# Order of the seven down products, and four smaller moves, in a decoder layer on eight cores

## The chip, the cores and the metric

One Trainium2 chip, all 8 cores; each core has 2048 of the 16384 tokens. The metric is the device time of the slowest core in microseconds (us). Some executions fall in a slower state in which one die (cores 0 to 3 or 4 to 7), or both, gets a lower granted TensorE clock, whatever the kernel; these are left out of every comparison ("fast runs" are the others). Ratios are the mean time of one kernel's fast runs over that of the other's of the same rounds; the medians quoted are of all runs, slow ones too, so the ratios are not quite theirs.

## The reference, cut to what matters

```python
def swiglu(x, w_up, w_down):
    gate, up = jnp.split(jnp.einsum('bsd,df->bsf', x, w_up), 2, axis=-1)
    return jnp.einsum('bsf,fd->bsd', jax.nn.silu(gate) * up, w_down)

def reference(...):                      # one layer: D_MODEL 2048, D_FF 5632, SEQ 16384
    mix = token_mixer(x, ...)            # projections, dilated attention A, sliding window B, w_out
    x = layer_norm(ALPHA * x + mix, ln1_g, ln1_b)
    x = layer_norm(ALPHA * x + swiglu(x, w_up, w_down), ln2_g, ln2_b)
```

The kernel works through two halves of its tokens (st) and, in each, two halves of the inner width (g): an up stage of 22 steps, then a down stage of 8 steps. So there are four down stages; they are called first to fourth here. Each product of a pair of weight blocks with the tokens is done by a scheme of seven products in place of eight; their operands are block sums (P, Q, R) of the weights.

## The kernel before

One down step p: banks BA, BB, BC, BD of PSUM take the products, VectorE adds them into the four z tiles q11 to q22, and also makes the sums P, Q, R of the next step's weights. Products 5 and 2 use P, 1 uses Q, 7 and 6 use R; 4 and 3 use the raw weights.

```python
# slots of the raw weight tiles (1408 KB each) of steps 0 to 7
D_OFF = [WB + (24576, 13312, 0)[i] for i in (0, 1, 2, 0, 1, 2, 1, 0)]

def wdone(k, key):                       # the raw weights of a step are no longer needed
    k.wlive = [e for e in k.wlive if e[0] != key]
    wfill(k)                             # issue further loads, in order, as far as slots are free

for p in range(5 if last else KC // 2):
    ...
    nxq = load_xq(p + 1) if p < 7 else None          # z tiles of the next step, a ring of five pairs
    ...
    P("5", BB, True, True, cs)
    P("1", BD, True, True, cs)
    P("4", BA, True, True, cs)
    acc(q11, BB, ALU.subtract, True)
    acc(q22, BB, ALU.subtract, True)
    acc(q11, BD)
    acc(q22, BD)
    acc(q21, BA, ALU.add, True)
    P("2", BC, True, True, cs)
    acc(q21, BC)
    if p < 7:
        d_sums(st, g, p + 1, "P")
        d_sums(st, g, p + 1, "Q")
    elif g == 0:
        u_sums(st, FG, "P")
    P("3", BB, False, True)
    wdone(k, key)
    acc(q12, BB, ALU.add, True)
    acc(q22, BB)
    P("7", BA, False, True)
    acc(q11, BA)
    if not last:
        store(0)
    P("6", BC, False, True)
    ...
    acc(q22, BC, ALU.subtract)
    if p < 7:
        d_sums(st, g, p + 1, "R")
    ...
    if g == 1:                           # LayerNorm sums: ACT squares, GpSimd adds twice per tile
        for i, q in ((2, q21), (1, q12), (0, q11), (3, q22)):
            stats(ss, i % 2, *q)
    if not last:
        store(1)
```

The softmax here doesn't subtract the row's maximum and nothing guards it: scores larger than these inputs give would overflow.

Of the kernel before, what the change touches and what calls it, by code (L numbers as in the profile page):

```python
# [43 lines left out]


class Op:
    __slots__ = ("eng", "fn", "deps", "is_dma", "semkey", "val", "needs_inc")


class Sched:  # L50
# [28 lines left out]
    def _add(self, eng, fn, reads, writes, joins=(), semkey=None):  # L79
        idx = len(self.ops)  # L80
        deps = set()
        for b in list(reads) + list(writes) + list(joins):
            for o in b.over:
                assert not o.ws, (b.name, o.name)
        for b in reads:
            deps.update(b.ws)
            if b.psum:
                deps.update(v for e, v in b.r.items() if e != eng)
        for b in list(writes) + list(joins):
            if b.prev:  # L90
                b.base |= self._old(b, set())
                b.prev = []
        for b in writes:
            deps.update(b.ws)
            deps.update(b.r.values())
            deps.update(b.rd)
            deps |= b.base
        for b in joins:
            deps |= b.base
            deps.update(b.r.values())  # L100
            deps.update(b.rd)
        op = Op()
        op.eng = eng
        op.fn = fn
        op.deps = deps
        op.is_dma = semkey is not None
        op.semkey = semkey
        op.val = 0
        op.needs_inc = False
        self.ops.append(op)  # L110
        for b in reads:
            if op.is_dma:
                b.rd.append(idx)
            else:
                b.r[eng] = idx
        for b in writes:
            b.base = set(b.ws) | set(b.r.values()) | set(b.rd)
            b.ws = [idx]
            b.r = {}
            b.rd = []  # L120
        for b in joins:
            b.ws.append(idx)
        return idx
# [10 lines left out]
    def pool(self, fn, reads, writes, joins=()):  # L134
        return self._add("pool", fn, reads, writes, joins)

    def dma(self, q, out, in_, reads, writes, semkey, joins=()):
        eng = {"sp": self.nc.sync, "pool": self.nc.gpsimd, "act": self.nc.scalar}[q]
        return self._add(q, lambda: eng.dma_start(out=out, in_=in_), reads, writes, joins, semkey=semkey)  # L139

    def emit(self, final_wait_ops):

# [9 lines left out]
        for i, op in enumerate(self.ops):  # L152
            e = op.eng
            w = []
            for d in sorted(op.deps, reverse=True):
                dop = self.ops[d]
                if not dop.is_dma and dop.eng == e and e == "pe":
                    continue
                if know[e] >> d & 1:
                    continue  # L160
                w.append(d)
                know[e] |= done[d]
            waits.append(w)
            for d in w:
                if not self.ops[d].is_dma:
                    self.ops[d].needs_inc = True
            if op.is_dma:
                done.append(know[e] | 1 << i)
                for j, (sem, last, val) in enumerate(free[e]):
                    if know[e] >> last & 1:  # L170
                        free[e].pop(j)
                        break
                else:
                    sem, val = nsem, 0
                    nsem += 1
                op.semkey, op.val = sem, val + 16
                free[e].append((sem, i, val + 16))
            else:
                issued[e] |= 1 << i
                done.append(know[e] | issued[e])  # L180
# [188 lines left out]
def phase1(k):  # L369
# [60 lines left out]
    load_x(1, (2, 2, 4, 4, 4))  # L430
    for h in range(8):
        S_.dma("pool", wk[h], k.wk_d[h], [], [bwk[h]], "wk%d" % h)
    for q in range(4):
        S_.dma("pool", wv[:, 4 * q:4 * q + 4, 1024:1152], k.wv_d[4 * q:4 * q + 4, :, 1024:1152].rearrange("c p n -> p c n"), [], [], "wvb",
               joins=[bwvb])
    S_.dma("pool", wkb, k.wkb_d, [], [bwkb], "wkb")
    k.bvs, k.bka, k.bkb = [], [[] for _ in range(8)], []
    later = []
# [173 lines left out]
def phase2(k):  # L612
# [47 lines left out]
    def load_kv(h):  # L660
# [8 lines left out]
        vt = vt.rearrange("p (b d) -> p b d", d=128)  # L669
        col = slice(h * 128, h * 128 + 128)  # L670
        first = [True]

        def ld(out, in_):
            S_.dma("sp", out, in_, k.bvs, [bv_] if first[0] else [], "va%d" % (h % 2), joins=[] if first[0] else [bv_])
            first[0] = False
        own = k.vs_d[TOK - 128:2 * TOK, col]
        ld(vt[:, 0:17, :], own.rearrange("(b p) d -> p b d", p=128))
# [329 lines left out]
    for u in range(32):  # L1007
# [3 lines left out]
            spend = [a_S(0, 0, 2, 0), a_S(0, 0, 1, 1)]  # L1011
        b_PV(j, kq, pend)
        b_evac(j, kq)
        run(peq, 1)
        proj(u + LEAD)
        run(dveq, 4)
        if u == 3:
            load_a()
# [181 lines left out]
def phase3(k):  # L1200
# [27 lines left out]
    def stats(ss, hh, z, bz):  # L1228
        (za, bza), (qa, bqa) = ss["accs"][hh]
        if hh not in ss["started"]:  # L1230
            ss["started"].add(hh)
            S_.act(lambda: nc.scalar.activation(out=qa, in_=z, func=AF.Square), [bz], [bqa])
            S_.pool(lambda: nc.gpsimd.tensor_copy(out=za, in_=z), [bz], [bza])
            return
        sq, bsq = ss["sq"][nxt("sq", len(ss["sq"]))]
        S_.act(lambda: nc.scalar.activation(out=sq, in_=z, func=AF.Square), [bz], [bsq])  # L1236
        S_.pool(lambda: nc.gpsimd.tensor_tensor(out=za, in0=za, in1=z, op=ALU.add), [bz, bza], [bza])  # L1237
        S_.pool(lambda: nc.gpsimd.tensor_tensor(out=qa, in0=qa, in1=sq, op=ALU.add), [bsq, bqa], [bqa])  # L1238

    def finish(ss, hh, bk0, both=False):  # L1240
        (za, bza), (qa, bqa) = ss["accs"][hh]
        (mu, bmu), (rs, brs) = ss["stat"][hh]
        tb, btb = ss["tt"][nxt("tt", len(ss["tt"]))]
# [79 lines left out]

    for st in range(2):
        zz = {}
        ss = open_stats("o%d" % st, [misc(9 + i) for i in range(4)], [misc(6), misc(7)], [misc(8)]) if st == 0 else ss
        ss["started"] = set()
        if st == 0:
            open_accs(ss, "o", [misc(i) for i in range(4)])
# [102 lines left out]
    def last_pairs(st, ss, zr, xq5, load_xq, acc, bhl):  # L1432
# [13 lines left out]
        def half_sum(p, o):  # L1446
# [3 lines left out]
            S_.dve(lambda: nc.vector.tensor_tensor(out=v, in0=w[:, 0:NJ, 0:128], in1=w[:, 0:NJ, 128:256], op=ALU.subtract), [bw], [b])  # L1450
            halls[p, "6"] = ([v[:, c, :] for c in range(NJ)], b)

        def stats_dve(hh, z, bz):
            (za, bza), (qa, bqa) = ss["accs"][hh]
            sq, bsq = ss["sq"][nxt("sq", len(ss["sq"]))]
# [4 lines left out]
        SB = ((4, 6), (0, 2))  # L1460
        stat = [None, None]

        def sums_out(hh):
            b0, b1 = SB[hh]
            for (a, ba), bk in zip(ss["accs"][hh], (b0, b1)):
                S_.pe(lambda a=a, bk=bk: nc.tensor.matmul(bank(k, bk), k.onesf, a, start=True, stop=True), [ba, k.bonesf], [k.bBK[bk]])
            mu, bmu = slot("mu%dl" % hh, xslot(hh))
            stat[hh] = [(mu, bmu), None]
            S_.act(lambda: nc.scalar.activation(out=tb, in_=bank(k, b0), func=AF.Square, scale=1.0 / D), [k.bBK[b0]], [btb])
# [38 lines left out]
        for p in (5, 6, 7):  # L1508
# [30 lines left out]
            if p < 7:  # L1539
                stats(ss, 0, *q11)  # L1540
                d_sums(st, g, p + 1, "R")
        stats_dve(0, *q[7][0])()

        dv = [(0, n) for n in range(13)] + [(1, n) for n in range(11)]
# [8 lines left out]
        for i, (p, m, bk) in enumerate(((5, "3", 0), (5, "6", 2), (6, "3", 1), (6, "6", 3), (7, "3", 5), (7, "6", 7))):  # L1553
            q11, q12, q21, q22 = q[p]
            prod(p, m, bk, p == 5, True)
            if m == "3":
                acc(q12, bk)
                acc(q22, bk)
                stats(ss, 1, *q12)
                if i == 0:  # L1560
                    sums_out(0)
                    ln(2)
                    rstd(0)
                ln(2)
            else:
                acc(q22, bk, ALU.subtract)
                if p < 7:
                    stats(ss, 1, *q22)
                    ln(3)
                else:  # L1570
                    tail = stats_dve(1, *q22)
                    ln(1)
                    tail()
        sums_out(1)
        ln(3)
        rstd(1)
        pend = None
# [12 lines left out]
    for st in range(2):  # L1590
        for g in range(2):
# [125 lines left out]
            for p in range(5 if last else KC // 2):  # L1717
# [18 lines left out]
                    S_.dma("sp", k.z2s_d[n, :, st * TS:(st + 1) * TS], view(k, wslot((n + 3) % 5 * 2), 1024, F32),  # L1736
                           [xq[2 * i][1], xq[2 * i + 1][1]], bz, "z2o")
                if p == 0:
                    for i, bk in (("5", BB), ("1", BD), ("4", BA), ("2", BC)):
                        P(i, bk, True, False, range(NJ - 1))  # L1740
                cs = [NJ - 1] if p == 0 else None
                P("5", BB, True, True, cs)
                P("1", BD, True, True, cs)
                P("4", BA, True, True, cs)
                acc(q11, BB, ALU.subtract, True)
                acc(q22, BB, ALU.subtract, True)
                acc(q11, BD)
                acc(q22, BD)
                acc(q21, BA, ALU.add, True)
                P("2", BC, True, True, cs)  # L1750
                acc(q21, BC)
                if p < 7:
                    d_sums(st, g, p + 1, "P")
                    d_sums(st, g, p + 1, "Q")
                elif g == 0:
                    u_sums(st, FG, "P")
                P("3", BB, False, True)
                wdone(k, key)
                acc(q12, BB, ALU.add, True)
                acc(q22, BB)  # L1760
                P("7", BA, False, True)
                acc(q11, BA)
                if not last:
                    store(0)
                P("6", BC, False, True)
                if p == 7 and g == 0:
                    u_sums(st, FG, "Q")
                acc(q22, BC, ALU.subtract)
                if p < 7:
                    d_sums(st, g, p + 1, "R")  # L1770
                elif g == 0:
                    u_sums(st, FG, "R")
                if g == 1:
                    for i, q in ((2, q21), (1, q12), (0, q11), (3, q22)):
                        stats(ss, i % 2, *q)
                if not last:
                    store(1)
                if st == 0 and g == 1:
                    if p == 0:
# [167 lines left out]
```

## Time and profile before

Median 2862.45 us (2856.41 to 3098.93 in 3 runs). What matters of the profiled run, whose slowest core is core 4:

| | us |
|---|---|
| span; PE busy; PE idle | 2861.7; 2745.7; 116 |
| the four up stages | 262, 273, 262, 273 |
| the four down stages, first to last z add | 131.9, 141.5, 129.0, 136.3 |
| PE waits inside them | 4.9, 13.7, 2.9, 4.9 |

The way to read it: PE is busy 96% of the span, so only what makes PE wait, or makes its matmuls slower, moves the time. The timeline, the stage table and the sums of VectorE that the argument rests on are shown in the prediction. One view more, PE's waits (us in total, times, longest):

```profile
PE sp L1382 <- DVE arena L1715: 14.9, 8, 5.2
PE sp L1382 <- DVE arena L1713: 6.5, 5, 1.7
PE sp L1382 <- DVE arena L1395: 4.9, 4, 2.1
...
PE sp L1247 <- POOL arena L1237: 3.5, 1, 3.5
```

L1382 are the matmuls of the up and down stages; L1715 and L1713 are VectorE's adds into z, L1395 is the block sum P. All told, the down stages hold PE up for 26 us.

### The profile page before, as it was taken

The numbers are of one execution on the slowest core, as the hardware profiler recorded it, in microseconds if no ns is written. First come the engines' busy times: TensorE is split into PE (matmuls) and PEld (weight loads), VectorE is DVE, ScalarE is ACT, GpSimd is POOL, SyncE is SP. The second block draws the span as 40 slices with busy tenths as digits, with TensorE's granted clock in tenths as the row PEclk, the third lists the DMA queues.
The fourth block names the chain that finished last, engine by engine and source line by source line (L and its number), as shares of the span: only waits on it lengthen the run. The fifth ranks groups of instructions, "written<-read, shape, count | busy, mean of one in ns | idle before, by whom it ended". The sixth has DMA issues, their size and how long they took to land.

```text
span 2861.7 us, 41480 instructions; the slowest of 8 cores (2850.4 to 2861.7 us)
## 1 busy us (share of the span) xinstructions
PE 2745.7 (96%) x14966; PEld 1319.8 (46%) x15077; DVE 1978.0 (69%) x2707; ACT 738.3 (26%) x1077; POOL 574.3 (20%) x571
## 2 busy tenths in 40 slices
PE   6999999998999999899999999998999999999995
PEld 2445555444666444344444444443444444444442
DVE  0744555788788826688865666676888765666787
ACT  0000000676666327333200112211333200212115
POOL 4000000122111555511100000046200000000166
PEclk9999999999999999999999999999999999999997
DMA  9974113556656758799989755599899799555863
GB/s 158 187 140 101 62 54 87 114 107 131 150 131 173 208 144 209 150 148 153 157 149 190 144 87 87 99 199 200 163 173 173 123 196 178 102 89 89 158 123 118
DMA packets 250810, 400.59 MB, mean 140 GB/s; under 512 B 89072, under 2 KB 127088, under 8 KB 249840
## 3 DMA queue, kind: packets, MB, share of 16 engines
q0 software_dynamic: 94272, 186.43, 43.7%
q1 hardware_dynamic: 141936, 182.12, 22.9%
q10 hardware_dynamic: 14400, 29.37, 3.4%
q8 instruction: 123, 2.02, 0.3%
q14 instruction: 79, 0.65, 0.1%
HBM read 491.42 MB, written 97.06 MB: 206 GB/s over the span
## 4 chain that ended last, share of the span: by engine, by line
PE 79%; DMA 9%; DVE 4%; issue 4%; ACT 2%; POOL 1%; ACTq 0%; DVEq 0%; POOLq 0%; SPq 0%
PE sp L1382 47%; PE sp L482 8%; PE sp L729 7%; PE sp L469 6%; PE sp L1194 4%; DMA arena<-wdn 2%; DMA z2s<-arena 2%; DMA arena<-z2s 1%; DMA arena<-wup 1%; DMA arena<-wv 1%; DMA arena<-x1s 1%; PE sp L538 1%; POOL arena L139 1%; PE sp L771 1%; ACT arena L358 1%
## 5 line engine op out<-in xcount | busy, mean ns | idle before, releaser
L1382 PE MATMUL sp<-arena 128*128 128x512 f16 x7408 | 1606.7, 380 | 31.7 <-DVE arena L1715 14.9
L1382 PEld LDWEIGHTS sp<-arena 128*128 128x128 f16 (+1 forms) x7408 | 723.8, 98 | 915.1 <-issue 50.5
L1632 DVE TENSOR_TENSOR arena<-sp,arena 128x512 f32<-128x512 f32 (+1 forms) x348 | 236.7, 689 | 159.1 <-PE sp L1382 143.9
L1715 DVE TENSOR_TENSOR arena<-arena,sp 128x512 f32<-128x512 f32 x257 | 166.6, 683 | 99.1 <-PE sp L1382 79.6
L729 PE MATMUL sp<-arena 128*128 128x512 bf16 x976 | 227.0, 381 | 5.4 <-ACT arena L358 2.2
L139 POOL DMA_DIRECT2D arena<-wup x88 | 65.9, 749 | 791.0 <-DVE arena L1395 491.1
L1194 PE MATMUL sp<-arena 128*128 128x512 bf16 x1003 | 220.7, 379 | 3.7 <-DVE arena L1359 1.5
L482 PE MATMUL sp<-arena 128*128 128x512 bf16 x1001 | 220.1, 379 | 1.2
L451 DVE TENSOR_TENSOR arena<-sp,arena 128x384 bf16<-128x384 f32 (+1 forms) x81 | 48.1, 606 | 200.8 <-PE sp L469 119.9
L1403 DVE TENSOR_TENSOR arena<-arena 128x2048 f16<-128x2048 bf16 (+1 forms) x118 | 186.8, 1583 | 0.0
L469 PE MATMUL sp<-arena 128*128 128x384 bf16 (+1 forms) x1036 | 182.4, 337 | 0.4
L1395 DVE TENSOR_TENSOR arena<-arena 128x2048 f16<-128x2048 bf16 (+1 forms) x118 | 156.6, 1327 | 34.4 <-DMA arena<-wdn 25.0
L1237 POOL TENSOR_TENSOR arena<-arena 128x512 f32<-128x512 f32 x118 | 161.0, 1365 | 74.9 <-DVE arena L1715 49.3
L1238 POOL TENSOR_TENSOR arena<-arena 128x512 f32<-128x512 f32 x118 | 157.9, 1338 | 25.6 <-ACT arena L1236 25.6
L1666 ACT ACTIVATE arena<-sp 128x512 f32<-128x512 f32 x86 | 51.5, 598 | 421.5 <-PE sp L1382 421.5
L1194 PEld LDWEIGHTS sp<-arena 128*128 128x128 bf16 x1024 | 100.0, 98 | 124.7 <-issue 5.2
L1236 ACT ACTIVATE arena<-arena 128x512 f32<-128x512 f32 x118 | 74.5, 632 | 317.1 <-DVE arena L1715 187.8
L482 PEld LDWEIGHTS sp<-arena 128*128 128x128 bf16 x1024 | 100.1, 98 | 120.3
L1632 DVE TENSOR_TENSOR arena<-arena 128x512 f16<-128x512 f32 (+1 forms) x304 | 154.8, 569 | 0.0
L358 ACT ACTIVATE arena<-sp,arena 128x512 bf16<-128x512 f32 (+1 forms) x37 | 24.7, 668 | 504.2 <-PE sp L502 429.0
L729 PEld LDWEIGHTS sp<-arena 128*128 128x128 bf16 x1024 | 97.7, 98 | 116.3 <-issue 6.5
L469 PEld LDWEIGHTS sp<-arena 128*128 128x128 bf16 x1040 | 101.7, 98 | 79.5
(143 smaller groups left out, 2510.7 us busy)
## 6 DMA issues: line engine op xcount, KB each, us to landing
arena<-wup POOLq DMA_DIRECT2D x88, 1024.0 KB, 11.3
arena<-wdn POOLq DMA_DIRECT2D x32, 1408.0 KB, 18.8
z2s<-arena SPq DMA_DIRECT2D x48, 512.0 KB, 12.4
arena<-wob SPq DMA_DIRECT2D x32, 512.0 KB, 5.9
arena<-xres SPq DMA_DIRECT2D x32, 512.0 KB, 7.8
x1s<-arena ACTq DMA_DIRECT2D x64, 256.0 KB, 7.0
arena<-x1s SPq DMA_DIRECT2D x32, 512.0 KB, 13.6
arena<-z2s SPq DMA_DIRECT2D x32, 512.0 KB, 17.4
```

The costliest lines, as they stand in the source:

```text
L139: return self._add(q, lambda: eng.dma_start(out=out, in_=in_), reads, writes, joins, semkey=semkey)
L469: ins = nc.tensor.matmul(bank(k, bk)[:, 0:c1 - c0], x[:, kc, blk * 128:blk * 128 + 128], wv[:, kc, c0:c1], start=(kc == 0), stop=(kc == KC ...
L482: ins = nc.tensor.matmul(bank(k, bk), wk[h][:, kc, :], x[:, kc, :], start=(kc == 0), stop=(kc == KC - 1))
L729: ins = nc.tensor.matmul(bank(k, bk), w[:, kc, :], x[:, kc, :], start=(kc == 0), stop=(kc == KC - 1))
L1194: ins = nc.tensor.matmul(bank(k, bk), w[:, kc, :], y[:, kc, hh * 512:(hh + 1) * 512], start=(first and i == 0), stop=(last and i == len(kc ...
L1237: S_.pool(lambda: nc.gpsimd.tensor_tensor(out=za, in0=za, in1=z, op=ALU.add), [bz, bza], [bza])
L1238: S_.pool(lambda: nc.gpsimd.tensor_tensor(out=qa, in0=qa, in1=sq, op=ALU.add), [bsq, bqa], [bqa])
L1382: ins = nc.tensor.matmul(bank(k, bk), w, x, start=(first and i == 0), stop=(last and i == len(ws) - 1), skip_group_check=True)
L1395: S_.dve(lambda: nc.vector.tensor_tensor(out=v, in0=w[:, 0:n, :], in1=w[:, n:2 * n, :], op=ALU.add), [bw], [b])
L1403: S_.dve(lambda: nc.vector.tensor_tensor(out=v, in0=w[:, :, 0:128], in1=w[:, :, 128:256], op=ALU.subtract), [bw], [b])
L1632: S_.dve(lambda: nc.vector.tensor_tensor(out=o, in0=a, in1=b, op=op), [ba, bb], [bo])
L1715: S_.dve(lambda: nc.vector.tensor_tensor(out=v, in0=v, in1=o, op=op), [b, bo], [b])
```

## The change

The intent: let VectorE add sooner, and let GpSimd's LayerNorm sums fall between VectorE's block sums, with which they contend. Four smaller moves go with it. The core of the diff:

```diff
-                P("5"), P("1"), P("4")   | acc q11 BB, q22 BB, q11 BD, q22 BD, q21 BA
-                P("2")                   | acc q21 BC; sums P, Q
-                P("3"); wdone            | acc q12 BB, q22 BB
-                P("7")                   | acc q11 BA; store(0)
-                P("6")                   | acc q22 BC; sums R; all four stats; store(1)
                 (the lines above are shortened; those below are the new code)
+                P("5", BB, True, True, cs)
+                P("2", BC, True, True, cs)
+                acc(q11, BB, ALU.subtract, True)
+                acc(q22, BB, ALU.subtract, True)
+                P("4", BA, True, True, cs)
+                acc(q21, BC, ALU.add, True)
+                sums("P")
+                P("1", BD, True, True, cs)
+                acc(q21, BA)
+                stat(0, q21)
+                P("7", BA, False, True)
+                acc(q11, BD)
+                acc(q22, BD)
+                sums("Q")
+                P("6", BC, False, True)
+                acc(q11, BA)
+                stat(0, q11)
+                P("3", BB, False, True)
+                wdone(k, key)
+                acc(q22, BC, ALU.subtract)
+                sums("R")
+                acc(q12, BB, ALU.add, True)
+                acc(q22, BB)
+                stat(1, q12)
+                stat(1, q22)
+                if not last:
+                    store(0)
+                    store(1)
 # LayerNorm sums: the add of the square is held until the next tile
-        S_.pool(lambda: nc.gpsimd.tensor_tensor(out=qa, in0=qa, in1=sq, op=ALU.add), [bsq, bqa], [bqa])
+        flush(ss)
+        ss["pend"] = [lambda: S_.pool(lambda: nc.gpsimd.tensor_tensor(out=qa, in0=qa, in1=sq, op=ALU.add), [bsq, bqa], [bqa])]
 # out projection: two square buffers, one temporary (was: one and two)
-        ss = open_stats("o%d" % st, [misc(9 + i) for i in range(4)], [misc(6), misc(7)], [misc(8)]) if st == 0 else ss
+        ss = open_stats("o%d" % st, [misc(9 + i) for i in range(4)], [misc(6)], [misc(8), misc(7)]) if st == 0 else ss
 # B: the rotation matmul of the unit before, inside the next projection
-        run(peq, 1)
-        proj(u + LEAD)
+        proj(u + LEAD, mid=lambda: run(peq, 1))
 # the loads of one V tile share one semaphore (group), which counts up to 16 times their number
-                op.semkey, op.val = sem, val + 16
+                val += 16 * len(group)
+                for m in group:
+                    self.ops[m].semkey, self.ops[m].val = sem, val
```

Left out: the tail, where a table load moves ahead and the sums of the last tile but one go straight to PE, without an add by GpSimd.

## The prediction

> **What bounds the kernel now.** I read the page first, then the busy time by stage, then the waits of PE, then the timeline of each stage that the change touches.
>
> ```profile
> PE 2745.7 (96%) x14966; PEld 1319.8 (46%) x15077; DVE 1978.0 (69%) x2707; ACT 738.3 (26%) x1077; POOL 574.3 (20%) x571
> 1210.00:1452.00 242.00, 240.96 (x1117) 108.97 (x1116) 207.66 (x308) 74.71 (x112) 31.92 (x52) 1.00 0.94 147
> 1452.00:1591.00 139.00, 133.96 (x618) 59.94 (x617) 83.41 (x109) 1.23 (x2) 6.68 (x9) 1.00 0.95 181
> 1857.00:2017.00 160.00, 146.34 (x664) 64.98 (x663) 109.20 (x115) 21.36 (x34) 92.76 (x71) 0.98 0.94 195
> 2280.00:2414.00 134.00, 131.05 (x606) 58.73 (x605) 82.47 (x108) 0.63 (x1) 6.63 (x9) 1.00 0.91 182
> 2683.00:2795.00 112.00, 107.09 (x489) 47.81 (x487) 88.89 (x92) 14.53 (x23) 62.53 (x48) 0.98 0.70 144
> ```
>
> The first line says that PE has 116 us of idle time in 2861.7; nothing else can give much. The others are stages (start:end, length, busy us of PE, weight load, DVE, ACT, POOL, granted clock, DMA share). The second is an up stage, for comparison; the last four are the down stages, one per half of the tokens and half of the inner width. They lack 5, 14, 3 and 5 us of PE work, and the first three run with the DMA engines 91 to 95% busy. The rest of the idle time is elsewhere: 19 us at the start, some 11 in attention of group B, 13 around the end of the out projection, some 20 in the tail.
>
> A down stage is eight steps p of seven products of 11 matmuls. At 217 ns each (10.74 us per 49 in the chain) a product is 2.39 us and a step 16.7. VectorE adds each product into four z tiles and makes the block sums P, Q, R of the next step's weights. These lines of the timeline show what a step waits for:
>
> ```profile
> 1465.89 100.24 PE L1382 MATMUL sp<-arena 128*128 128x512 f16 x462 [0.96 <-DVE arena L1713]
> 1535.64 1.48 POOL L139 DMA_DIRECT2D arena<-wdn  x2 [32.49 <-PE sp L1382]
> 1554.70 1.62 DVE L1395 TENSOR_TENSOR arena<-arena 128x2816 f16<-128x2816 bf16 x1 [4.62 <-DMA arena<-wdn]
> 1473.95 1.62 DVE L1403 TENSOR_TENSOR arena<-arena 128x2816 f16<-128x2816 bf16 x1
> 1895.34 7.54 DVE L1403 TENSOR_TENSOR arena<-arena 128x2816 f16<-128x2816 bf16 x1
> 1926.17 35.22 PE L1382 MATMUL sp<-arena 128*128 128x512 f16 x154 [5.17 <-DVE arena L1715]
> ```
>
> First: step 0 begins with a wait of 0.96 us. Second and third: GpSimd issues the weights of steps 6 and 7 together (x2) when step 4 lets go of its slot, and P of step 6 (L1395) can start 19.1 us later, when the first has landed. The same pair took 17.7 us (2364.25 to 2381.96) and 21.7 us (1947.82 to 1969.58) in the other two stages. Fourth and fifth: the same sum R takes 1.62 us alone and 7.54 us while GpSimd runs the LayerNorm sums back to back. Sixth: PE idles 5.17 us for a z tile loaded late, and its next 9 matmuls start every 0.43 us, then every 0.21: such an idle costs about 1.9 us more.
>
> **What the Trainium skill says.** "SBUF — State Buffer", Who interferes with whom: a VectorE instruction with two SBUF inputs contends with a GpSimd instruction that reads SBUF. The 1.62 against 7.54 us agrees. "TensorE: Matmul & The Clock Gate", Part 1: an idle window of about 3.4 us halves the clock. The trace agrees after 5.17 us idle, and shows no such start after 2.06. "DMA: Bandwidth & Descriptors", Issuing engines are not separate DMA queues: all queues interleave on the same 16 engines. The 17.7 to 21.7 us for one weight tile in the busy stages agree; in the last stage, with those queues quiet, both tiles of the pair were through in about 22 us.
>
> **The change part by part.**
>
> *Rotation of B inside the next projection.* It removes PE's waits on the bias copy of ACT (L358): 4.2 us at L362 and 2.2 at L729. But the period is not set by PE:
>
> ```profile
> 573.18 1.93 ACT L778 ACTIVATE arena<-sp 128x1024 bf16<-128x1024 f32 x2
> 574.99 0.70 ACT L834 ACTIVATE arena<-sp,arena 128x512 f32<-128x512 f32 x1
> 575.78 0.63 ACT L835 ACTIVATE arena<-arena 128x512 f32<-128x512 f32 x1
> 576.51 1.01 DVE L838 TENSOR_TENSOR arena<-sp,arena 128x512 bf16<-128x512 f32 x1 [0.61 <-ACT arena L835]
> 577.67 0.63 ACT L824 ACTIVATE arena<-arena 128x512 f32<-128x512 bf16 x1 [1.26 <-DVE arena L838]
> 578.21 0.67 ACT L358 ACTIVATE arena<-sp,arena 128x512 bf16<-128x512 f32 x1
> 578.78 1.93 ACT L778 ACTIVATE arena<-sp 128x1024 bf16<-128x1024 f32 x2
> ```
>
> From 573.18 to 578.78 each starts when the one before ends: a closed loop of ACT and DVE of 5.60 us, while PE alone needs 5.32 (its period before the loop has caught up, 523 to 535 us). The order on ACT does not change, so the loop stays; PE will wait for L838, whose bank PV overwrites, instead of L358. Worth 0.3 us.
>
> *V semaphore group.* The order of instructions shows that the first PV of each A head goes from six or seven DMA semaphores to one. In the trace that PV starts 0.75 us after the matmuls before it at the beginning of a head, 0.48 otherwise: 8 x 0.27 = 2 us, on PE, which bounds that stage. Gain 2.
>
> *Statistics of the out projection.* Two square buffers and a deferred add. GpSimd there waits for ACT, which is packed (3 LayerNorm pieces and 2 squares per pair of tiles, 7.85 us), so about one add of 1.25 us comes off the backlog that PE waits for near 1187. Gain 1.2.
>
> *Tail.* The exp table load of 1.28 us moves ahead (DVE idles 1.01 us for it), and the last sums need one GpSimd pair less. VectorE's 24 tiles still set the end. Gain 1.5.
>
> *Down order 5 2 4 1 7 6 3.* This frees VectorE: sums of GpSimd now fall in the gaps between P, Q and R, so the 7 us sums go. In the second of the four down stages that is worth some 2 us, in the last stage the 3.95 us that PE waited at 2782.92 plus 1.9 of slow clock. It costs three things.
>
> (a) Product 7 overwrites the bank of 4, whose add now stands behind P of the next step on VectorE. In step 0 only the last chunk of 5, 2, 4, 1 is left, so PE reaches 7 at once and waits for five VectorE instructions (starts 0.6 apart, P 1.6): 3.8 us in place of 0.96. Four stages: +11.
>
> (b) The raw weights are used by 4 and 3. The order moves 3 from fifth to last, so the slot is let go 2 x 2.39 = 4.8 us later. For steps 3 to 5 there is a spare step. Step 6 uses the slot of step 4: its load starts at the end of step 4 and lands 17.7 to 21.7 us later, and by (a) product 7 of step 5, due 9.5 us after that end, needs it plus P and one add (2.6 us). Stall 17.7 + 2.6 - 9.5 = 10.8, 12.2, and 14.8 us: 38 for the three stages, + 3 x 1.9 of slow clock = 44. In the last stage the tile lands in some 13.5 us (my estimate from the pair's 22): stall 6.6 plus clock, against 3.95 plus clock: +3. In return the stalls that steps 6 and 7 have now (4.0, 0.7 and 6.7 us) mostly go, because the loads get time: -8.
>
> (c) The first store of a step moves from after product 7 in sixth place to the end, 3.1 us later, and the load that reuses its slot follows; and a late z tile now blocks 3.1 us sooner. From the issue of that store to the landing of the load took 20 to 28 us in the first and third down stages (1488.29 to 1514.47: 26.2) and up to 32 in the second. The chain has little slack at 26, but the pair of stores and the loads will overlap less with the next step's: +4, guessed between 0 and 20.
>
> Sum: + 11 + 44 + 3 - 8 + 4 - 2 = + 52 for the down stages (the last stage's gain is already in its +3), - 5 for the rest: +47. 2862 + 47 = 2909.
>
> **The rivals.** *Contention was the bound*: spreading the GpSimd sums cures the stalls of the third and last stages, 14 + 5 us, and the load of step 6 hides; with B's 6 us that would be 2840. For it: the 7.5 us sums and the slow clock after them. Against: in the first and third down stages no GpSimd sums run, and L1395 already waits for the weights in all three. *PE bounds B*: then 23 periods x 0.3 = 6 us more gain; against it the closed loop. *The z chain runs away*: with 26 us of store and load in every step, every second step stalls 5 us or more, and the stages take 20 to 25 us longer each, with the slow clock: 2940. *The DMA is quicker when PE stalls*, since nothing else is asked for: the pair's 22 us in the quiet stage gives 11 to 13 us for a tile; then (b) is 5 to 6 us per stage and the total 2885.
>
> **Range and chances.** The last two rivals give 2885 and 2940; I take 2880 to 2938. 2% slower is 2919.7, a little inside: slower 0.30. Faster by 2% would need 57 us, half of PE's idle time: 0.01.
>
> **What would show it.** In step 5 of the first three down stages one PE wait of 10 to 15 us ahead of the fifth product, on a VectorE add that stands behind P, which itself waits for wdn; half-rate matmuls after it; a wait of about 3.8 us at each stage's start; R at 1.6 to 2.7 us everywhere; B's period at 5.6 with the wait on L838. I am wrong if P of step 6 finds its weights there, if step 5 does not stall, or if B's period falls to 5.3.

## The result, and the profile after

Median 2953.03 us (2952.12 to 3284.42 in 4 runs), against 2860.25 for the kernel before beside it: ratio 1.0328, 95% interval 1.0304 to 1.0351. It is slower by 93 us, where 47 were predicted; the range ended at 2938.

The first line of the page, then the four down stages (start:end, length, busy us of PE, weight load, DVE, ACT, POOL, granted clock, DMA share, GB/s), bounded by their first and last z add:

```profile
PE 2772.2 (94%) x15081; PEld 1324.5 (45%) x15081; DVE 1942.2 (66%) x2707; ACT 737.0 (25%) x1078; POOL 565.8 (19%) x569
```

```profile
1467.90:1622.90 155.00, 130.81 (x583) 57.72 (x581) 81.98 (x104) 0.00 (x0) 5.92 (x8) 0.92 0.84 158
1896.40:2065.80 169.40, 134.53 (x583) 58.53 (x581) 80.93 (x102) 19.30 (x31) 78.81 (x66) 0.88 0.81 166
2346.00:2506.60 160.60, 131.80 (x583) 58.04 (x581) 82.08 (x104) 0.00 (x0) 5.92 (x8) 0.91 0.79 154
2780.10:2922.60 142.50, 130.14 (x581) 57.56 (x578) 94.91 (x119) 27.47 (x44) 75.47 (x61) 0.96 0.50 111
```

The stages are 23.1, 27.9, 31.6 and 6.2 us longer than before, 88.8 together. The up stages take 262, 273, 261 and 273 us as before. What is left is 2 us: the first up stage begins 3.7 us later, and the tail after the last z add is 1.0 us shorter (30.2 against 31.2). So the loss is in the down stages. Within them the granted clock (0.92, 0.88, 0.91, 0.96) was 0.98 to 1.00 before: it is low where PE has waited. PE's waits:

```profile
PE sp L1400 <- DVE arena L1746: 98.8, 14, 21.6
...
PE sp L1265 <- POOL arena L1249: 8.3, 1, 8.3
...
PE sp L1265 <- POOL arena L1251: 2.8, 2, 1.6
```

One line has taken the place of three: every wait in the down stages now ends with the same add of z (L1746), and all 14 stand before product 7. The timeline of the first down stage shows the two kinds. Step 0 and the next slow matmuls:

```profile
1469.67 1.62 DVE L1413 TENSOR_TENSOR arena<-arena 128x2816 f16<-128x2816 bf16 x1
1471.20 1.87 DVE L1746 TENSOR_TENSOR arena<-arena,sp 128x512 f32<-128x512 f32 x3
1472.03 4.52 PE L1400 MATMUL sp<-arena 128*128 128x512 f16 x13 [3.69 <-DVE arena L1746]
```

P of the next step (L1413) stands ahead of the add that PE waits for: 3.69 us, the same in all four stages (predicted 3.8). And 13 matmuls take 4.52 us in place of some 2.8: the slow clock. The clock records of the traces show when it comes. Between full and half speed the clock changes only at marks 3.41 us apart, which lie elsewhere on each core. In all 13 traces kept, on all eight cores, from 30 to 2700 us, a stretch at full clock with more than 2.06 us of PE idle between two marks was always followed by half clock until the next mark, and one with less than 1.87 us never was. So the place of a wait counts as well as its length. A wait of 2.49 us in step 2 fell almost wholly between two marks (columns as in the stage table above):

```profile
1507.39:1510.80 3.41, 1.20 (x6) 0.61 (x7) 3.41 (x5) 0.00 (x0) 0.00 (x0) 1.00 1.07 244
1510.80:1514.21 3.41, 3.41 (x10) 1.21 (x8) 1.34 (x2) 0.00 (x0) 0.00 (x0) 0.50 1.04 104
```

Step 5:

```profile
1553.87 1.48 POOL L140 DMA_DIRECT2D arena<-wdn  x2 [33.84 <-PE sp L1400]
1554.08 0.92 SPq L140 DMA_DIRECT2D z2s<-arena  x2
1555.09 2.99 SPq L140 DMA_DIRECT2D arena<-x1s  x2
...
1577.11 1.63 DVE L1413 TENSOR_TENSOR arena<-arena 128x2816 f16<-128x2816 bf16 x1 [18.35 <-DMA arena<-wdn]
1578.65 1.88 DVE L1746 TENSOR_TENSOR arena<-arena,sp 128x512 f32<-128x512 f32 x3
1579.48 5.74 PE L1400 MATMUL sp<-arena 128*128 128x512 f16 x19 [16.77 <-DVE arena L1746]
```

The chain is the one foretold: release of the slot, load, P, add, product 7. But P starts 23.2 us after the issue of the tile, not 17.7 to 21.7. In the second and third stages it is 28.1 and 25.1 us, and PE waits 21.64 and 18.61. On the eight cores the three times are 20.8 to 23.9, 24.3 to 28.9 and 21.6 to 25.7 us; in the kernel before they were 14.5 to 19.1, 18.5 to 23.5 and 14.4 to 17.7. The second and third lines hold the reason that the experiments confirm: the stores of z and the loads of the next z now start at the same moment as the pair of weight tiles. In the kernel before, the first store came 3.4 us after the weights (1535.64 and 1539.09).

The PE waits by kind, in us, first to fourth stage:

| | before | after | gain or loss |
|---|---|---|---|
| step 0 | 0.96 in each | 3.69 in each | +10.9 |
| step 5: weights of step 6 by way of P | | 16.77, 21.64, 18.61 | +57.0 |
| same, fourth stage | 3.95 | 7.36 | +3.4 |
| steps 5 to 7, other | 3.95, 7.35, 0.67 | none | -12.0 |
| steps 1 to 4: z tiles late | 0, 5.34, 1.28 | 3.74, 9.41, 6.49 | +13.0 |
| sum of waits | | | +72.3 |
| rest of the 88.8: slower matmuls after waits | | | +16.5 |

The last line is what remains. The clock records give nearly the same by themselves: in the four stages the half clock cost a busy PE 22.5 us after and 3.6 before, 18.9 more.

The stage that ends the out projection went otherwise than foretold as well. Before, two sums of VectorE over the tokens' blocks were blocked by GpSimd's LayerNorm sums, which were not slowed:

```profile
1174.58 18.18 DVE L1281 TENSOR_TENSOR arena<-arena 128x2048 f16<-128x2048 f16 x2
```

After, the same two are quick, but three GpSimd adds take 2.2 us in place of 1.26 (one is shown), and the square of the first half is added only with the last tile:

```profile
1172.93 7.05 DVE L1299 TENSOR_TENSOR arena<-arena 128x2048 f16<-128x2048 f16 x2
...
1176.72 2.17 POOL L1249 TENSOR_TENSOR arena<-arena 128x512 f32<-128x512 f32 x1
...
1190.58 2.93 POOL L1251 TENSOR_TENSOR arena<-arena 128x512 f32<-128x512 f32 x2
```

GpSimd is done at 1193.5 in place of 1190.5, and PE, there 3.5 us earlier than before, waits 8.3 and 1.6 us for it in place of 3.5.

In B the period is 5.60 us as before (adds at 576.86 and 582.46; before 576.51 and 582.11). The sums R (L1403, now L1421) took up to 7.99 us before and 1.93 at most after.

### The profile page after: what moved, and what is told of

Read it like the earlier page. It is cut to its first block, busy times and chain, and to the rows that moved or that the text cites. A ratio compares the mean times of both kernels' runs of the same rounds, so it can differ in the third digit from the quotient of the medians.

```text
span 2952.8 us, 41503 instructions; the slowest of 8 cores (2932.4 to 2952.8 us)
## 1 busy us (share of the span) xinstructions
PE 2772.2 (94%) x15081; PEld 1324.5 (45%) x15081; DVE 1942.2 (66%) x2707; ACT 737.0 (25%) x1078; POOL 565.8 (19%) x569
## 3 DMA queue, kind: packets, MB, share of 16 engines
q1 hardware_dynamic: 141936, 182.12, 22.5%
## 4 chain that ended last, share of the span: by engine, by line
PE 79%; DMA 9%; DVE 4%; issue 4%; ACT 2%; POOL 1%; DVEq 0%; ACTq 0%; SPq 0%; POOLq 0%
PE sp L1400 48%; PE sp L494 7%; PE sp L742 6%; PE sp L481 6%; PE sp L1206 5%; DMA arena<-wdn 4%; DMA arena<-x1s 1%; DMA arena<-wv 1%; PE sp L550 1%; DVE arena L1746 1%; DMA arena<-z2s 1%; POOL arena L140 1%; ACT arena L791 1%; PE sp L514 0%; PE sp L947 0%
## 5 line engine op out<-in xcount | busy, mean ns | idle before, releaser
L1400 PE MATMUL sp<-arena 128*128 128x512 f16 x7408 | 1624.3, 383 | 100.5 <-DVE arena L1746 98.8
L1746 DVE TENSOR_TENSOR arena<-arena,sp 128x512 f32<-128x512 f32 x257 | 168.9, 683 | 172.8 <-PE sp L1400 148.6
L742 PE MATMUL sp<-arena 128*128 128x512 bf16 x1024 | 236.9, 379 | 3.8 <-DVE arena L375 1.5
L1206 PE MATMUL sp<-arena 128*128 128x512 bf16 x1024 | 222.1, 379 | 3.3 <-DVE arena L1377 1.8
L494 PE MATMUL sp<-arena 128*128 128x512 bf16 x1024 | 222.2, 379 | 0.0
L1413 DVE TENSOR_TENSOR arena<-arena 128x2048 f16<-128x2048 bf16 (+1 forms) x118 | 161.6, 1369 | 70.0 <-DMA arena<-wdn 70.0
L1249 POOL TENSOR_TENSOR arena<-arena 128x512 f32<-128x512 f32 x117 | 153.9, 1315 | 158.7 <-DVE arena L1746 125.9
L1251 POOL TENSOR_TENSOR arena<-arena 128x512 f32<-128x512 f32 x117 | 155.8, 1333 | 18.8 <-ACT arena L1248 15.5
L1421 DVE TENSOR_TENSOR arena<-arena 128x2048 f16<-128x2048 bf16 (+1 forms) x118 | 158.3, 1342 | 0.0
```

The lines of the kernel that those rows point to most:

```text
L494: ins = nc.tensor.matmul(bank(k, bk), wk[h][:, kc, :], x[:, kc, :], start=(kc == 0), stop=(kc == KC - 1))
L742: ins = nc.tensor.matmul(bank(k, bk), w[:, kc, :], x[:, kc, :], start=(kc == 0), stop=(kc == KC - 1))
L1206: ins = nc.tensor.matmul(bank(k, bk), w[:, kc, :], y[:, kc, hh * 512:(hh + 1) * 512], start=(first and i == 0), stop=(last and i == len(kc ...
L1249: S_.pool(lambda: nc.gpsimd.tensor_tensor(out=za, in0=za, in1=z, op=ALU.add), [bz, bza], [bza])
L1251: ss["pend"] = [lambda: S_.pool(lambda: nc.gpsimd.tensor_tensor(out=qa, in0=qa, in1=sq, op=ALU.add), [bsq, bqa], [bqa])]
L1400: ins = nc.tensor.matmul(bank(k, bk), w, x, start=(first and i == 0), stop=(last and i == len(ws) - 1), skip_group_check=True)
```

## The experiments

Theory S: the loss of step 5 is made of a slot let go late and a product that needs the tile early, each of them half. Rival Z: late z tiles and their traffic are the cause. Stages are in the order first to fourth; "landing" is the time from the issue of the weights of step 6 to the start of P on them.

### Everything but the down loop

```diff
 # open: the changed kernel, its down loop replaced by that of before
-                P("5"), P("2"), P("4"), P("1"), P("7"), P("6"), P("3"); wdone
+                P("5"), P("1"), P("4"), P("2"), P("3"); wdone; P("7"), P("6")
```

> The changed kernel with the down loop of before (order 5 1 4 2 3 7 6, stores and sums as before); all other parts of the change stay. My prediction gave these other parts -5 us: time 2855. The traces of the two kernels say otherwise: the out projection is reached 3.5 us earlier (B, V), but its LayerNorm sums end 3 us later and the up stage starts 3.4 us late (1205.9 against 1202.2), and the tail is 1 us shorter: +2, time 2862 to 2864. If the slowdown of 93 us is not in the down loop, this run would stay above 2900. The four down stages should go back to 132, 141, 129 and 136 us from first to last z add.

Two of five runs were fast, 2871.4 and 2871.7; ratio to before 1.0000 (0.9917 to 1.0083). The stages took 131.9, 144.7, 128.5 and 136.1 us, landing 17.0, 26.9, 16.8. The 26.9 came with the old order: in the second stage of this run the cores spread from 19.7 to 26.9, so more than the order moves a landing. But the loss is gone. So the down loop holds it, and the rest of the change is worth nothing that these runs resolve; the -5 of the prediction lies within the noise.

### The down loop alone

```diff
 # the kernel before, with the changed down loop and nothing else
```

> The kernel before with the changed down loop and nothing else of the change. If the down loop is the whole cause: the four down stages take 153 to 155, 164 to 169, 153 to 160 and 139 to 143 us as in the changed kernel, and the time is 85 to 90 us above before, about 2950. If the other parts (deferred sums, V group, rotation) made part of the slowdown by acting together with it: clearly less, below 2930.

Median 2956.0, ratio 1.0291 (1.0229 to 1.0354). Stages 158.8, 171.6, 156.7, 144.4; waits of step 5 16.95, 21.06, 17.79; landing 23.4, 27.5, 24.3. The down loop alone does it, with the other parts absent.

### The slots of steps 6 and 7 exchanged

```diff
-D_OFF = [WB + (24576, 13312, 0)[i] for i in (0, 1, 2, 0, 1, 2, 1, 0)]
+D_OFF = [WB + (24576, 13312, 0)[i] for i in (0, 1, 2, 0, 1, 2, 0, 1)]
```

> The changed kernel, but the weights of down step 6 lie in the slot of step 3 and those of step 7 in the slot of step 4 (before: the other way round). Slot theory (the wait of step 5 is for a tile whose slot was let go too late): tile 6 loads a step earlier, the PE waits of 16.8, 21.6 and 18.6 us in step 5 vanish, and that of 7.4 in the last stage too; the second weight tile of the following up stage now shares memory with step 7 and comes late, 3 stages x about 6 us. Time about 2953 - 57 - 7 - 6 (clock) + 18 = 2900. Rival (the late z tiles and the traffic of their stores and loads are what holds step 5): the waits of step 5 stay above 10 us, time above 2930.

The waits of step 5 for weights and that of 7.4 us in the fourth stage are gone. On core 4 product 7 still waits 3.69 us in step 0 of each stage and up to 8.65 us for z (in step 5 of the second stage). The next up stage waits 3.9 and 3.8 us for its second weight tile, and the second 2.5. But the time of the fast runs was 2931 to 2951 us, ratio 1.0246 (1.0172 to 1.0321), verdict unclear. In the profiled run the cores took from 2876 (core 3) to 2944 us (core 4), and the trace shows two reasons. The waits for z differ: beyond step 0, PE waits 12.1 us in the down stages of core 3 and 37.5 in those of core 0 (2928 us); it was 19.6 in the changed kernel. And some cores lose clock while PE is busy. The same stretch on core 4 and on core 3 (columns as before):

```profile
2090.00:2170.00 80.00, 79.53 (x304) 32.76 (x302) 60.93 (x91) 21.47 (x32) 4.45 (x6) 0.81 0.64 131
2090.00:2170.00 80.00, 80.00 (x373) 36.27 (x371) 71.38 (x107) 27.00 (x40) 4.44 (x6) 1.00 0.85 175
```

By the clock records cores 4 and 5 ran 158 us at 0.8125 of full speed from 2011 us on, cores 6 and 7 163 us from 1194 us on, and cores 0 to 3 not at all. Such a stretch costs some 30 us (estimated: 158 x 0.1875), in a run that still counts as fast. Cores 0 to 3, without it, took 2876 to 2928 us around the 2900 of theory S. So theory S is right on the wait that it named, and z traffic, the rival's cause, takes part of the gain back. What starts such a stretch no run shows.

### Product 3 in fifth place

```diff
                 P("1", BD, True, True, cs)
                 acc(q21, BA)
                 stat(0, q21)
+                P("3", BB, False, True)
+                wdone(k, key)
+                acc(q11, BD)
+                acc(q22, BD)
+                sums("Q")
                 P("7", BA, False, True)
-                ...
-                P("6", BC, False, True)
-                ...
-                P("3", BB, False, True)
-                wdone(k, key)
+                acc(q12, BB, ALU.add, True)
+                acc(q22, BB)
+                ...
+                P("6", BC, False, True)
+                ...
```

> The changed kernel with product 3 in fifth place (5 2 4 1 3 7 6), so the weights are let go 2 products (4.8 us) earlier and product 7 is due one product (2.4 us) later; P still stands before the add that product 7 waits for. Slot theory: each step 5 wait falls by 7.2 us to about 9.6, 14.4 and 11.4; that of the last stage from 7.4 to 0; the wait of step 0 from 3.7 to 1.3 without slow clock (-16 for four stages). The z waits of steps 2 to 4 (19.6 us and clock) go too if they come from the late first store, because z12 is again finished in fifth place and z11 before the last product: time 2884. If they stay: 2908. If the cause of the slowdown is elsewhere: above 2930.

Median 2873.4, ratio 1.0003 (0.9939 to 1.0067): the whole loss is gone, some 11 us more than theory S expected (2884). Step 5 waits 2.84, 6.07 and 3.28 us instead of 9.6, 14.4 and 11.4, because the landing is shorter as well: 16.4, 19.7 and 16.9 us. In the first stage:

```profile
1544.60 1.48 POOL L140 DMA_DIRECT2D arena<-wdn  x2 [35.79 <-PE sp L1400]
1547.18 2.76 SPq L140 DMA_DIRECT2D z2s<-arena  x2
...
1561.03 1.62 DVE L1413 TENSOR_TENSOR arena<-arena 128x2816 f16<-128x2816 bf16 x1 [6.80 <-DMA arena<-wdn]
```

The weights are issued 2.6 us before the stores, not 0.2. So the place of product 3 does three things: it frees the slot sooner, puts product 7 later, and takes the weights' load out of the way of z. The third was in neither theory.

### The add of bank 4 ahead of P

```diff
                 acc(q21, BC, ALU.add, True)
-                sums("P")
-                P("1", BD, True, True, cs)
                 acc(q21, BA)
                 stat(0, q21)
+                sums("P")
+                P("1", BD, True, True, cs)
```

> The changed kernel with the add of bank 4 ahead of the block sum P of the next step on VectorE; order of products and release of the slot as changed. Theory (half of the step 5 wait is that product 7 needs the next weights by way of P): product 7 no longer waits for weights; what remains is product 5 of step 6, due 16.7 us after the release, with weights after 23.2 and P 1.6: wait 8.1, 13, 10 instead of 16.8, 21.6, 18.6 (-26). Step 0 waits 2.1 instead of 3.7 and without slow clock after it (-13 for four). Last stage's 7.4 goes (-7). z waits of steps 2 to 4 fall by up to 1.6 each (-8). Time about 2899. If only the late release matters, the waits move to step 6 at full length: 2935 or more.

The waits came as expected: step 0 2.42 us (2.1 expected), and the wait for weights in step 6 8.12, 12.06, 8.00 (8.1, 13, 10 expected). The wait of 7 us in the fourth stage stayed (7.13), against expectation: that stage does its last steps in code of its own, which the edit doesn't touch. From the timeline of core 7:

```profile
1470.07 33.40 PE L1400 MATMUL sp<-arena 128*128 128x512 f16 x154 [2.42 <-DVE arena L1746]
...
1576.69 63.53 PE L1400 MATMUL sp<-arena 128*128 128x512 f16 x281 [8.12 <-DVE arena L1413]
```

The one run counted as fast took 2939.5 us, but its cores 6 and 7 had a stretch of 161 us at 0.8125 of the clock (an up stage of 261 us took 279.5 there, with PE always busy). The other six cores took 2879 to 2912 us, against 2899 expected and 2932 to 2953 in the changed kernel: a gain, of one run. The landing remained 22 to 26 us, since the z stores still start with the weights.

### z transfers moved in the program

```diff
+                late = not last
-                nxq = load_xq(p + 1) if p < 7 else None
+                nxq = load_xq(p + 1) if p < 7 and not (late and p == 5) else None
 ...
+                if late and p == 4:
+                    held = [lambda f=store: f(0), lambda f=store: f(1)]
+                elif late:
+                    if p == 5:
+                        for f in held: f()
+                        nxq = load_xq(6)
+                    store(0); store(1)
```

> For measuring, not for speed: the changed kernel, with the z stores of step 4 and the z loads of step 6 held back to the end of step 5 in the first three down stages, so that no z transfer starts beside the weights of steps 6 and 7. In the changed kernel the first of these tiles was usable 23.2, 28.1 and 25.1 us after its issue, with z requests 0.2 us behind it; where they come 2.6 us behind it (before; product 3 fifth) 16.4 to 21.8. If the simultaneous z traffic is the cause of the extra 5 to 7 us: 16 to 18 us here in the first and third stages, waits of step 5 of 10 to 12 us in place of 16.8 and 18.6. If not: 22 to 25 as in the changed kernel. Step 6 then waits for its late z tiles instead, so the total stays near 2950.

It failed as an experiment: 2953.6 us, landing 24.4, 28.9 and 24.1, and the stores still start 0.2 us after the weights. Here the queue sent each transfer as soon as what it waited for was done; its later place in the program didn't hold it back. It served as a repeat of the changed kernel.

### z transfers held by a real dependence

```diff
-                def store(i, p=p, xq=xq):
+                def store(i, p=p, xq=xq, after=()):
 ...
-                           [xq[2 * i][1], xq[2 * i + 1][1]], bz, "z2o")
+                           [xq[2 * i][1], xq[2 * i + 1][1], *after], bz, "z2o")
 # and the held stores of step 4 are given the last z tile of step 5 as something that they wait for
```

> The experiment with held z transfers, mended: moving their issue in the program had changed nothing, because the queue sends each as soon as its tiles are ready. Now the z stores of step 4 wait for the last add of step 5, and the z loads of step 6 stand behind them in their queue. If the simultaneous z traffic makes the weights of step 6 late: first tile usable 16 to 18 us after issue in the first and third down stages (23.2 and 25.1 in the changed kernel), about 20 in the second (28.1), and waits of step 5 of about 10, 13 and 11 us in place of 16.8, 21.6 and 18.6. If the DMA is just as slow without them: 22 to 25 us as there. Step 6 and 7 then wait for late z tiles, so the total says nothing.

Landing 13.2, 17.5 and 14.0 us in place of 23.2, 28.1 and 25.1; waits of step 5 6.71, 11.00 and 7.48. On the eight cores they are 10.6 to 14.0, 13.3 to 17.6 and 10.2 to 14.0 us, all below the lowest of the changed kernel. The traffic of z thus makes the weights 10 to 11 us late, more than expected. First stage:

```profile
1550.13 1.48 POOL L140 DMA_DIRECT2D arena<-wdn  x2 [32.44 <-PE sp L1400]
1563.30 1.63 DVE L1413 TENSOR_TENSOR arena<-arena 128x2816 f16<-128x2816 bf16 x1 [8.29 <-DMA arena<-wdn]
1565.67 18.72 PE L1400 MATMUL sp<-arena 128*128 128x512 f16 x77 [6.71 <-DVE arena L1746]
1576.36 0.80 SPq L140 DMA_DIRECT2D z2s<-arena  x2
```

The rate of the DMA tells the size. From issue to landing in the first stage (start:end, length, POOL busy, granted clock, DMA share, GB/s), the changed kernel, the kernel with product 3 fifth, and this one:

```profile
1553.80:1577.10 23.30, 1.48 (x2) 0.75 0.96 167
```

```profile
1544.60:1561.00 16.40, 1.48 (x2) 1.00 0.93 166
```

```profile
1550.10:1563.30 13.20, 1.48 (x2) 0.98 0.86 128
```

Length times rate gives 3.9, 2.7 and 1.7 MB carried before P can start. The tile itself is 1408 KB, 1.44 MB. The two stores and two loads of z are 4 x 512 KB, 2.1 MB. The trace counts the bytes of each queue: that of z carried 2.08, 1.09 and 0 MB in these stretches, that of the weights 1.81, 1.62 and 1.67 (the start of the second tile is in it). (In this run step 6 then waits 15 us for its z, as it must: 2965 us in all.)

### Both halves: product 3 fifth and the add first

```diff
 # the two edits above together: sums("P") after acc(q21, BA), and P("3") with wdone in fifth place
```

> Product 3 fifth and the add of bank 4 ahead of block sum P, together: the two halves of the step 5 wait both taken away. The run with 3 fifth still waited 2.8, 6.1 and 3.3 us at product 7 (P and its weights in front of the add). Here product 7 waits for no weights, and product 5 of step 6 is due 21.5 us after the release, with weights after 16.5 to 20 and P 1.6: no wait but a few us in the second stage. Theory (late release and early need are two separate halves): 8 to 12 us less than with 3 fifth alone, about 2860, no different from before. If the order of the adds cures nothing more once the weights come early: 2870.

Median 2856.9, ratio 0.9965 (0.9887 to 1.0044). Stages 131.4, 139.3, 127.9, 133.4. Step 0 waits 0.96 us, as before. The weights of step 6 cost 1.66 us in the second stage and nothing in the others.

### The LayerNorm sums of before

```diff
 # the changed kernel with the down loop of before, and:
-        ss = open_stats("o%d" % st, [misc(9 + i) for i in range(4)], [misc(6)], [misc(8), misc(7)]) if st == 0 else ss
+        ss = open_stats("o%d" % st, [misc(9 + i) for i in range(4)], [misc(6), misc(7)], [misc(8)]) if st == 0 else ss
-        flush(ss)
-        ss["pend"] = [lambda: S_.pool(lambda: nc.gpsimd.tensor_tensor(out=qa, in0=qa, in1=sq, op=ALU.add), [bsq, bqa], [bqa])]
+        S_.pool(lambda: nc.gpsimd.tensor_tensor(out=qa, in0=qa, in1=sq, op=ALU.add), [bsq, bqa], [bqa])
```

> The changed kernel with the down loop of before and also the LayerNorm sums of before (two temporaries and one square buffer, second add at once): what remains is B's rotation inside the projection, the V semaphore group and the tail. If the deferred add lengthens the end of the out projection, as the traces say (last sums 1190.5 before, 1193.5 after, although PE came 3.5 us earlier): about 5 us less than the run with the old down loop alone, PE's wait there 1 to 5 instead of 8 us plus 1.6; 3 to 5 us faster than before. My prediction had the deferred add as a gain of 1.2: then 1 us more than that run.

Fast runs 2860.4 and 2862.0, ratio 0.9969 (0.9869 to 1.0069). PE waits 5.15 us for the sums, in place of 8.07 and 1.61 in the run with the deferred add. Where these sums were put back, VectorE's two sums took over 17 us again (17.8 here, 17.4 in the combination below). The trace speaks for a loss of some 4 us by the deferred add; the times, at 0.3 to 1%, can't tell.

### The combination of what helps

```diff
 # product 3 fifth, add of bank 4 first, LayerNorm sums of before; rotation, V group and tail as changed
```

> Product 3 fifth, add of bank 4 first, LayerNorm sums as before, and the rest of the change: everything that the traces show as a loss is out. If the reckoning holds: 5 us below the run with both, 2855, some 0.2% below before, which is within the noise (same).

> The best combination again (product 3 fifth, add of bank 4 ahead of P, LayerNorm sums as before, rest of the change), with more rounds. From its first runs: 0.5% below before, 2851 to 2860 us. If that was luck of the chip's state, the interval will hold 1.0 again with its centre at 0.998 or above.

Medians 2855.1 and 2859.6, ratios 0.9948 (0.9888 to 1.0009) and 0.9966 (0.9924 to 1.0008). Both point to 0.3 to 0.5% less than before, and both intervals hold 1.0. It has the lowest median of the versions tried, and is not shown to be faster than the kernel before.

## Why the prediction was wrong

- **The bound, the place and the direction** were right: PE is the bound, the loss is in the down stages, at product 7 of step 5, by way of P and the raw weights. Each of the two halves has its own experiment. Product 3 in fifth place alone takes the loss away (ratio 1.0003), because it also parts the weights from z; with the add first as well, the wait for the weights of step 6 is 1.66 us at most.
- **(a), product 7 behind P**: 3.69 us for 3.8, +10.9 for +11. The slow clock after it was not in the sum. In the first stage 154 matmuls after it took 35.09 us, against 33.40 at full rate: 1.7 us more, and 1.4 to 1.7 in the other stages, 6 us in all.
- **(b), the failed step**: the landing time of the weights of step 6, "its load starts at the end of step 4 and lands 17.7 to 21.7 us later". It landed after 23.2, 28.1 and 25.1 us, and the stalls were 57.0 us for the three stages instead of 38: +19. The 17.7 to 21.7 were taken from a trace in which the stores of z follow the weights by 2.6 to 3.4 us. The change moves those stores to the very end of the step, next to the release, and so puts 2.1 MB beside the tile. The prediction had seen the move under (c), but set it only against other z transfers ("the pair of stores and the loads will overlap less with the next step's"), not against the weights. With z held back the tile lands in 13.2, 17.5 and 14.0 us; that settles it. The rival of a DMA that is quicker while PE stalls was also half right, 13 us, but only with z out of the way.
- **(c), the z chain**: +13.0 by the table for +4, less the 2 that spread sums should have given back in the second stage: 11 too little. With product 3 fifth the first stage that had waited 3.7 waits 2.8, and with both edits nothing; that the late first store is the cause fits this, but no run moved that store alone.
- **Old stalls of steps 6 and 7**: -12.0 for -8. Right in kind.
- **Slow clock**: +16.5 net for 3 x 1.9 = 5.7. The prediction counted one slow start after each of the three waits of step 5; waits of 3.69 have it too, and some of 2.5 (see the marks above). An error of 11.
- **The fourth stage**: +3.4 for +3, right. With a quiet DMA its tile was there 13.8 us after issue (estimated 13.5).
- **The spread sums**: R at most 1.93 us, as foretold. It brought next to nothing: the one long wait that R of 7.99 us had stood before, 3.95 us in the fourth stage, gave way to the 7.36 us for the weights.
- **The rest**: -5 predicted, +2 by the traces. B at 5.60 us was right; the wait on L838 that was to show it did not come (PE's waits on L358 are gone, and six of at most 0.2 us on another VectorE line took their place). The deferred sum of the out projection was called a gain of 1.2 and is a loss of about 4 in the traces; the tail gained 1.0 for 1.5. The V group was not run by itself, so its 2 us stay open.

The down terms sum to 88.8 measured for the 52 predicted: 19 from the landing, 11 from the clock, 11 from the z chain, less 4 from old stalls. Two slips change nothing: the 217 ns of a matmul come from 33.40 us for 154, while 10.74 us for 49 would be 219; and in the first rival the stall of 14 us is that of the second down stage, not of the third.

## What to carry to other kernels

When an edit moves a buffer's release, look at what else starts at that moment afterwards: the landing time read in the old trace belongs to the old neighbours. Bytes in flight over the rate of the stretch accounts for the three landings here after the fact; as a forecast it was not tried. Put the last user of a prefetched operand early in its step, and don't let the add that frees a bank stand behind work that waits for a load. A contention that is plain to see (7 us sums) is worth only what the bounding engine waits for it.

## What the Trainium skill lacked or had wrong

- "TensorE: Matmul & The Clock Gate", Part 1, names an idle window of about 3.4 us before the clock halves. The traces have the marks 3.41 us apart, but PE need not be idle all the time between two: at full clock, more than 2.06 us of idle there always brought half clock, and less than 1.87 us never did (13 traces, eight cores each). So a wait of 2.49 us that fell between two marks did (154 matmuls in 35.09 us, 33.40 at full rate), and one of 2.95 us that a mark cut into 1.7 and 1.2 did not (core 1 of the run with the old down loop).
- "TensorE: Matmul & The Clock Gate", Part 1, also tells of a limit that takes a whole die to 13/16 of the clock. Here stretches of 158 to 163 us at 0.8125 took cores 4 and 5, or 6 and 7, and left the other two cores of the die at full clock at that time, in two runs. That it is the same limit no run shows.
- "DMA: Bandwidth & Descriptors", Issuing engines are not separate DMA queues, says that transfers interleave, which agrees. That section does not size the delay. Here 1408 KB landed after 13.2, 16.4 and 23.2 us, with 0, 1.09 and 2.08 MB of another queue carried meanwhile, at 128, 166 and 167 GB/s in all.
- "SBUF — State Buffer", Who interferes with whom: that issue order decides who blocks agrees with the out projection (VectorE's two sums 18.18 us and GpSimd's adds 1.26, then 7.05 and 2.2 after one add was deferred). Not there, but seen here: relieving VectorE lengthened GpSimd's chain by 3 us (done at 1193.5 in place of 1190.5).
